# Cross-entropy on one core: the first load as two transfers of even and odd partitions, both ahead of the opening barrier, and the labels by GpSimd's queue

## The chip, the core and the metric

The kernel runs on one core of a Trainium2 chip. The metric is the device time of one launch in microseconds (us). A profile of one execution of each kernel shows the span from its first to its last instruction, some 1.8 us shorter than the device time.

## The reference

```python
batch, num_classes = 256, 32000
log_probs = logits - max(logits, axis=-1)
log_probs = log_probs - log(sum(exp(log_probs), axis=-1))
out[i] = -log_probs[i, labels[i]]            # float32, 256 numbers
```

The logits are 32.77 MB of float32, read once. Everything else is small.

## The kernel before

Two rows of the batch lie in each of the 128 partitions, one after the other, 64000 columns in all. They are loaded in 14 chunks of falling width by the sync engine's queue (SP). ScalarE takes the exponential of each chunk as it lands, with its sum as by-product.

```python
CHUNKS = [1024, 15104, 12672, 8960, 7136, 4992, 3872, 2848, ...]   # 14 in all
SLOTS = [0, 1, 2, 3, 4, 5, 2]       # the first six have buffers of their own

def load(i):
    t, base = tiles[i]
    a, b = starts[i], starts[i] + CHUNKS[i]
    nc.sync.dma_start(out=t[:, a - base:b - base], in_=flat[:, a:b])
...
first = len(set(SLOTS))             # 6
for i in range(first):
    load(i)
nc.scalar.dma_start(out=lbl[:, :], in_=...)     # labels, 2 KB, ScalarE's hardware queue
nc.gpsimd.iota(out=idx[:, :], ...)
make_identity(nc, ident[:, :])
nc.gpsimd.tensor_add(out=idx[:, :], in0=idx[:, :], in1=lbl[:, 0:2 * ROWS:2])
for r in range(ROWS):
    nc.gpsimd.indirect_dma_start(out=g[:, r:r + 1], in_=logits[:, :], ...)   # the labels' logits
```

All engines meet at a barrier before the program's body begins. A function that runs when the program is finished takes the sync engine's first load out of the body and puts it ahead of that barrier:

```python
first = next(i for i in rest if i.engine == SP and i.opcode == "DMACopy")
rest.remove(first)
at = next(k for k, i in enumerate(head) if i.engine == SP and i.opcode == "Drain")
head.insert(at, first)              # cut: the two lists are stored back
```

The softmax here doesn't subtract the row's maximum and nothing guards it: scores larger than these inputs give would overflow.

Of the kernel before, what the change touches and what calls it, by code (L numbers as in the profile page):

```python
# [9 lines left out]
P = 128  # L10
# [19 lines left out]
def begin_first_load_before_barrier(nc):  # L30


    main, body = nc.m.functions[0].blocks[:2]
    rest = list(body.instructions)
    first = next(i for i in rest if i.engine == mybir.EngineType.SP and i.opcode == "DMACopy")
    rest.remove(first)
    head = list(main.instructions)
    at = next(
        k for k, i in enumerate(head) if i.engine == mybir.EngineType.SP and i.opcode == "Drain"
    )  # L40
    head.insert(at, first)
    main.instructions = head
    body.instructions = rest

# [2 lines left out]
def kernel(  # L47
# [5 lines left out]
):  # L53
    nc = tc.nc
    nc.at_finalize(begin_first_load_before_barrier)
    B, C = logits.shape
    assert B == P * ROWS and sum(CHUNKS) == ROWS * C


    flat = logits.rearrange("(p r) c -> p (r c)", r=ROWS)  # L60
# [4 lines left out]
    at = 0  # L65
# [43 lines left out]
    def load(i):  # L109
        t, base = tiles[i]  # L110
        a, b = starts[i], starts[i] + CHUNKS[i]
        nc.sync.dma_start(out=t[:, a - base:b - base], in_=flat[:, a:b])  # L112

    seen = [0] * ROWS

    def exps(i):
        t, base = tiles[i]
        for a, b, r in pieces[i]:
            if i == last:
                acc = s_last[:, :]  # L120
            else:
                acc = parts[r][:, seen[r]:seen[r] + 1]
                seen[r] += 1
            nc.scalar.activation(  # L124
                out=t[:, a - base:b - base],
                in_=t[:, a - base:b - base],
                func=AF.Exp,
                accum_out=acc,
            )

    def log_row(r):
        nc.scalar.activation(  # L132
            out=res[0:1, r:ROWS * P:ROWS], in_=lane[r][:, :], func=AF.Ln
        )

    with tc.manual_schedule():
        first = len(set(SLOTS))
        for i in range(first):
            load(i)

        nc.scalar.dma_start(
            out=lbl[:, :], in_=bass.AP(tensor=lbl_words, offset=0, ap=[[2 * ROWS, P], [1, 2 * ROWS]])
        )
        nc.gpsimd.iota(out=idx[:, :], pattern=[[C, ROWS]], base=0, channel_multiplier=ROWS * C)  # L144
# [3 lines that stand above are left out]
            nc.gpsimd.indirect_dma_start(  # L148
                out=g[:, r:r + 1],
                out_offset=None,  # L150
                in_=logits[:, :],
                in_offset=bass.IndirectOffsetOnAxis(ap=idx[:, r:r + 1], axis=1),
            )


        done = 0
        for i in range(first, len(CHUNKS)):
            slot = SLOTS[i] if i < TAIL else TAIL_SLOT
            while done <= SLOTS[:first].index(slot):
                exps(done)  # L160
                done += 1
            load(i)
        nc.scalar.activation(out=eg[:, :], in_=g[:, :], func=AF.Exp, scale=-1.0)  # L163
        for r in range(ROWS):
            nc.vector.tensor_scalar_mul(diag[r][:, :], ident[:, :], eg[:, r:r + 1])  # L165
        for i in range(done, last):
            exps(i)
            if i == turn:
                nc.vector.reduce_sum(out=sums[:, 0:1], in_=parts[0][:, :], axis=mybir.AxisListType.X)  # L169
                nc.tensor.matmul(lane[0][:, :], sums[:, 0:1], diag[0][:, :], start=True, stop=True)  # L170
            if i == turn + 1:
                log_row(0)
            if i == WARM_FROM:
                col = parts[1][:, seen[1] - 1:seen[1]]
                for _ in range(WARM):
                    nc.tensor.matmul(warm[:, :], col, diag[0][:, :], start=True, stop=True)  # L176
        nc.vector.reduce_sum(out=sums[:, 1:2], in_=parts[1][:, :], axis=mybir.AxisListType.X)  # L177
        nc.tensor.matmul(lane[1][:, :], sums[:, 1:2], diag[1][:, :], start=True, stop=False)  # L178
        exps(last)
        nc.tensor.matmul(lane[1][:, :], s_last[:, :], diag[1][:, :], start=False, stop=True)  # L180
        log_row(1)
        nc.sync.dma_start(
            out=out.rearrange("(a n) -> a n", a=2), in_=res[0:1, :].rearrange("o (a n) -> o a n", a=2)
        )
# [30 lines left out]
```

## Time and profile before

| | us |
|---|---|
| device time, median of six runs | 84.47 (84.29 to 84.98) |
| span of the profile | 82.6 |
| first load issued, first 4 KB packet moves | 0.00, 1.03 |
| second load (15104 columns) issued | 0.81 |
| exponentials of the first three chunks begin | 3.70, 21.58, 36.72 |
| ScalarE busy | 58.4 |

How to read it: up to 36.7 us the kernel is one stream of loads, after that ScalarE is nearly always busy, and what ScalarE does then starts when the stream's first large chunks have landed. The list of DMA issues gives, for each load, its size and the time from issue to landing (last number, us):

```profile
x<-in_logits_dram SPq DMA_DIRECT2D x1, 7552.0 KB, 20.7
...
x<-in_logits_dram SPq DMA_DIRECT2D x1, 512.0 KB, 3.7
```

The timeline of the sync engine in two short windows gives the issues themselves (start, us, what):

```profile
0.00 0.40 SPq L112 DMA_DIRECT2D x<-in_logits_dram  x1
...
0.81 0.80 SPq L112 DMA_DIRECT2D x<-in_logits_dram  x2
```

The first issue takes 0.40 us. The second row is two issues, the second and the third load, back to back.

### The profile page before, as it was taken

How to read it: one execution, taken by the hardware profiler on the slowest of the kernel's cores; microseconds unless marked ns; L12 is line 12 of the kernel's file. 1: busy time of each engine (PE TensorE's matmuls, PEld its weight loads, DVE VectorE, ACT ScalarE, POOL GpSimd, SP SyncE). 2: the span in 40 equal slices, each digit the busy share in tenths (PEclk: the TensorE clock that was granted, in tenths of full speed). 3: DMA queues.
4: the chain of work that ended last, by engine and by line, in shares of the span. 5: the costliest groups of instructions: out<-in, count | busy, mean ns of one | idle time of the engine just before them, and what ended most of it. 6: DMA issues, size and time to landing. Idle time of an engine off the chain costs nothing.

```text
span 82.6 us, 174 instructions
## 1 busy us (share of the span) xinstructions
PE 6.0 (7%) x30; PEld 2.9 (4%) x30; DVE 0.8 (1%) x4; ACT 58.4 (71%) x34; POOL 3.0 (4%) x10
## 2 busy tenths in 40 slices
PE   0000000000000000000000002000000000008970
PEld 0000000000000000000000000000000000005620
DVE  0000000000000000000000020000000000000000
ACT  6230000000599999629999999989999999999970
POOL 3000000000370000000000000000000000000000
PEclk9999999999999999999999999999999999999998
DMA  4999999678999999979899799999999999999800
GB/s 73 649 469 469 469 469 439 264 322 381 491 516 540 418 393 393 393 330 504 382 452 486 318 415 443 443 405 435 464 395 450 397 431 423 419 408 408 325 0 0
DMA packets 2226, 32.77 MB, mean 397 GB/s; under 512 B 433, under 2 KB 434, under 8 KB 1202
## 3 DMA queue, kind: packets, MB, share of 16 engines
q1 hardware_dynamic: 2018, 32.77, 93.4%
q10 hardware_dynamic: 144, 0.00, 0.1%
q0 software_dynamic: 64, 0.00, 0.1%
HBM read 32.77 MB, written 0.00 MB: 397 GB/s over the span
## 4 chain that ended last, share of the span: by engine, by line
DMA 43%; ACT 39%; issue 13%; PE 0%; SPq 0%; another core or an unknown queue 0%
DMA x<-in_logits_dram 43%; ACT x L124 27%; ACT x_tail L124 12%; ACT res L132 1%; PE lane L180 0%; SPq L112 0%; ACT eg L163 0%
## 5 line engine op out<-in xcount | busy, mean ns | idle before, releaser
L124 ACT ACTIVATE x<-x 128x1024 f32<-128x1024 f32 (+7 forms) x8 | 46.4, 5794 | 20.9 <-DMA x<-in_logits_dram 20.9
L124 ACT ACTIVATE x_tail<-x_tail 128x2848 f32<-128x2848 f32 (+6 forms) x7 | 9.8, 1404 | 0.0
L176 PE MATMUL warm<-diag,parts 128*1 128x128 f32 x24 | 4.7, 382 | 23.2 <-ACT x_tail L124 23.2
L170 PE MATMUL lane<-diag,sums 128*1 128x128 f32 x2 | 0.6, 397 | 50.8 <-DVE sums L169 50.8
L176 PEld LDWEIGHTS warm<-diag,parts 128*1 128x1 f32 x24 | 2.7, 115 | 25.4 <-ACT x_tail L124 23.7
L148 POOL DMA_INDIRECT g<-in_logits_dram,idx x2 | 2.1, 1036 | 0.6 <-issue 0.3
L170 PEld LDWEIGHTS lane<-diag,sums 128*1 128x1 f32 x2 | 0.1, 80 | 50.8 <-DVE sums L169 50.8
L103 ACT ACT_TABLE_LOAD x1 | 1.3, 1283 | 0.8 <-PEq L199 0.8
L124 ACT ACTIVATION_READ_ACCUMULATOR x<-x 128x1 f32 x8 | 1.5, 186 | 0.0
L124 ACT ACTIVATION_READ_ACCUMULATOR x_tail<-x_tail 128x1 f32 x7 | 1.3, 185 | 0.0
L165 DVE TENSOR_SCALAR diag<-ident,eg 128x128 f32<-128x128 f32 x2 | 0.5, 282 | 47.8 <-ACT eg L163 47.8
L146 POOL TENSOR_TENSOR idx<-idx,lbl 128x2 int32<-128x2 int32 x1 | 0.2, 193 | 20.2 <-DMA lbl<-in_labels_dram 20.2
L132 ACT ACTIVATE res<-lane 1x128 f32<-1x128 f32 x2 | 0.5, 265 | 0.5 <-PE lane L180 0.5
L177 DVE TENSOR_REDUCE sums<-parts 128x1 f32<-128x10 f32 x1 | 0.2, 163 | 28.4 <-ACT x_tail L124 28.4
L180 PE MATMUL lane<-diag,s_last 128*1 128x128 f32 x2 | 0.4, 270 | 0.1
L178 PE MATMUL lane<-diag,sums 128*1 128x128 f32 x2 | 0.4, 270 | 0.1
masks.py:199 POOL TENSOR_SCALAR_AFFINE_SELECT ident<-ident 128x128 f32<-128x128 f32 x1 | 0.3, 292 | 0.1
masks.py:197 POOL MEMSET ident<- 128x128 f32 x1 | 0.2, 194 | 0.0
L163 ACT ACTIVATE eg<-g 128x2 f32<-128x2 f32 x1 | 0.2, 187 | 0.0
L169 DVE TENSOR_REDUCE sums<-parts 128x1 f32<-128x4 f32 x1 | 0.2, 156 | 2.3 <-ACT x L124 2.3
L144 POOL IOTA idx<- 128x2 int32 x1 | 0.1, 120 | 0.5 <-POOLq L199 0.5
L199 POOL MEMSET const-uint8-127<- 128x1 uint8 x1 | 0.1, 118 | 0.0
(5 smaller groups left out, 0.5 us busy)
## 6 DMA issues: line engine op xcount, KB each, us to landing
x<-in_logits_dram SPq DMA_DIRECT2D x1, 7552.0 KB, 20.7
x<-in_logits_dram SPq DMA_DIRECT2D x1, 6336.0 KB, 35.5
x<-in_logits_dram SPq DMA_DIRECT2D x1, 4480.0 KB, 45.6
x<-in_logits_dram SPq DMA_DIRECT2D x1, 3568.0 KB, 53.6
x<-in_logits_dram SPq DMA_DIRECT2D x1, 2496.0 KB, 59.0
x<-in_logits_dram SPq DMA_DIRECT2D x1, 1936.0 KB
x_tail<-in_logits_dram SPq DMA_DIRECT2D x1, 1424.0 KB, 21.7
x_tail<-in_logits_dram SPq DMA_DIRECT2D x1, 1072.0 KB, 23.8
```

Source lines behind the costliest of these rows:

```text
L103: nc.scalar.preload_act_table_set("natural_log_exp_and_others")
L124: nc.scalar.activation(out=t[:, a - base:b - base], in_=t[:, a - base:b - base], func=AF.Exp, accum_out=acc,)
L132: nc.scalar.activation(out=res[0:1, r:ROWS * P:ROWS], in_=lane[r][:, :], func=AF.Ln)
L146: nc.gpsimd.tensor_add(out=idx[:, :], in0=idx[:, :], in1=lbl[:, 0:2 * ROWS:2])
L148: nc.gpsimd.indirect_dma_start(out=g[:, r:r + 1], out_offset=None, in_=logits[:, :], in_offset=bass.IndirectOffsetOnAxis(ap=idx[:, r:r + 1 ...
L163: nc.scalar.activation(out=eg[:, :], in_=g[:, :], func=AF.Exp, scale=-1.0)
L165: nc.vector.tensor_scalar_mul(diag[r][:, :], ident[:, :], eg[:, r:r + 1])
L169: nc.vector.reduce_sum(out=sums[:, 0:1], in_=parts[0][:, :], axis=mybir.AxisListType.X)
L170: nc.tensor.matmul(lane[0][:, :], sums[:, 0:1], diag[0][:, :], start=True, stop=True)
L176: nc.tensor.matmul(warm[:, :], col, diag[0][:, :], start=True, stop=True)
L178: nc.tensor.matmul(lane[1][:, :], sums[:, 1:2], diag[1][:, :], start=True, stop=False)
L180: nc.tensor.matmul(lane[1][:, :], s_last[:, :], diag[1][:, :], start=False, stop=True)
```

## The change

The intent: bring the first data in sooner by giving the 16 DMA engines half-loads to begin with, and bring the labels sooner by a queue of their own. The first load becomes two transfers of 64 partitions, even and odd; both are put ahead of the barrier; the labels go by GpSimd's software queue.

```diff
-    first = next(i for i in rest if i.engine == SP and i.opcode == "DMACopy")
-    rest.remove(first)
+    first = [i for i in rest if i.engine == SP and i.opcode == "DMACopy"][:2]
+    for i in first:
+        rest.remove(i)
...
-    head.insert(at, first)
+    head[at:at] = first
...
-        nc.sync.dma_start(out=t[:, a - base:b - base], in_=flat[:, a:b])
+        step = 2 if i == 0 else 1
+        for p in range(step):
+            nc.sync.dma_start(out=t[p:P:step, a - base:b - base], in_=flat[p:P:step, a:b])
...
-        nc.scalar.dma_start(
+        nc.gpsimd.dma_start(
             out=lbl[:, :], ...
```

More of the change, by code (lines that the diff above doesn't have):

```diff
@@ L34, in begin_first_load_before_barrier @@
     rest = list(body.instructions)
-    first = next(i for i in rest if i.engine == mybir.EngineType.SP and i.opcode == "DMACopy")
-    rest.remove(first)
+    first = [i for i in rest if i.engine == mybir.EngineType.SP and i.opcode == "DMACopy"][:2]
+    for i in first:
+        rest.remove(i)
     head = list(main.instructions)
```

## The prediction

> **What bounds the kernel now.** I read the chain of waits first, then the timeline, then the table of stretches, and only then the waits and issues of the small label transfer. The chain in order of time:
>
> ```profile
> 22 pieces in order of time: start us, us, what
> 0.81 0.33 SPq L112
> 1.14 0.05 issue
> 1.19 35.51 DMA x<-in_logits_dram
> 36.70 0.02 issue
> ...
> 55.51 0.25 another core or an unknown queue
> ...
> 69.93 9.84 ACT x_tail L124 x14
> ```
>
> Up to 36.70 us the chain is the stream of loads. After that it is ScalarE, exponential after exponential, with one more short wait at 55.51 us. The timeline shows the same waits at the instruction that waits:
>
> ```profile
> 3.70 1.06 ACT L124 ACTIVATE x<-x 128x1024 f32<-128x1024 f32 x1 [1.62 <-DMA x<-in_logits_dram]
> 21.58 12.79 ACT L124 ACTIVATE x<-x 128x15104 f32<-128x15104 f32 x1 [16.72 <-DMA x<-in_logits_dram]
> 36.72 10.76 ACT L124 ACTIVATE x<-x 128x12672 f32<-128x12672 f32 x1 [2.26 <-DMA x<-in_logits_dram]
> 55.78 6.15 ACT L124 ACTIVATE x<-x 128x7136 f32<-128x7136 f32 x1 [0.27 <-DMA x<-in_logits_dram]
> ```
>
> The number in brackets is idle time just before the instruction. The first exponential ends at about 4.8 us, and the engine then stands for 16.7 us until the second chunk lands: when the first chunk lands is of no use in itself. What counts is when the 15104, 12672 and 7136 columns have landed, and those three are points on one stream. Check: columns 1024 to 16128 are 7.73 MB, which landed in 21.58 - 3.70 = 17.9 us, 432 GB/s; the next 6.49 MB took 36.72 - 21.58 = 15.1 us, 429 GB/s; the next 8.24 MB took 19.06 us, 432 GB/s. The stream runs at one speed and never stops, so a stream that starts d earlier brings each of these landings, and the end, forward by d. The other way round as well.
>
> So the question is the start of the stream. The table of stretches (columns: window, its length, five engines' busy time, clock, DMA share, GB/s) shows it:
>
> ```profile
> 0.00:1.00 1.00, 0.00 (x0) 0.00 (x0) 0.00 (x0) 0.20 (x1) 0.29 (x6) 1.00 0.00 0
> 1.00:1.50 0.50, 0.00 (x0) 0.00 (x0) 0.00 (x0) 0.50 (x1) 0.42 (x3) 1.00 1.13 131
> 1.50:2.00 0.50, 0.00 (x0) 0.00 (x0) 0.00 (x0) 0.50 (x1) 0.05 (x1) 1.00 0.58 156
> 2.00:2.50 0.50, 0.00 (x0) 0.00 (x0) 0.00 (x0) 0.09 (x1) 0.00 (x0) 1.00 0.97 385
> 5.20:7.40 2.20, 0.00 (x0) 0.00 (x0) 0.00 (x0) 0.00 (x0) 0.00 (x0) 1.00 0.95 412
> ```
>
> Nothing moves for 1.0 us, and then the rate is low for another 1.0 to 1.5 us. From 1.0 to 2.5 us the three rows give 0.5 x (131 + 156 + 385) = 336 KB; at 432 GB/s it would have been 648 KB, so the ramp costs (648 - 336) / 432 = 0.72 us. (Later rows count a 60 KB packet where it starts, so the half-microsecond rows from 2.5 to 3.5 us are not rates.) The packet records of the trace say what the ramp is: the first 4 KB packets of the first load start from 1.03 us on, spread over about 0.4 us, and last 0.16 to 1.0 us each; from about 2.1 us on a packet lasts 0.159 us and they follow each other without a gap. The first packets of the second load start between 2.84 and 3.35 us, engine by engine, and the engine that begins it last ends it last: eight packets of 2.23 us make 3.35 into 21.2 us, and the exponential starts at 21.58. The latest engine of the ramp sets the time.
>
> **What the Trainium skill says.** "DMA: Bandwidth & Descriptors", section "Rules for kernel authors", says of two transfers to disjoint partition halves not to bother, as both are spread over the same 16 engines and serialize. That speaks against a gain in bandwidth, and I expect none: the stream already holds 432 GB/s here. The same page, "Queues, rings and completion order", says that a DMA engine takes turns between queues packet by packet. The trace agrees: the labels, 128 packets of 16 bytes on ScalarE's queue, lie one between each two 60 KB packets, and so land only with the second chunk (below). "Perfetto Trace Analysis", section "DMA Optimizations", says that splitting transfers may let some start sooner where DMA engines are idle; the first 2 us here are such a place. Its lifecycle of a hardware-generated DMA, section "DMA Instruction — HWDGE (DVE, Sync)", says that the generator is locked for one instruction at a time and shared between sequencers; no row of this trace shows that directly.
>
> **The change part by part.**
>
> 1. Two issues ahead of the barrier. In the instruction records the first issue takes 0.00 to 0.40 us, the sequencer's drain 0.45 to 0.58, the barrier's release reaches it at 0.73, and the second load is issued at 0.81. The timeline's issues on that queue last 0.33 to 0.50 us. A second issue therefore adds about 0.40 us (0.35 and a gap of 0.05), and every engine that waits at the barrier leaves it about 0.40 us later. ScalarE's table load (0.80 to 2.09) moves to about 1.20 to 2.49, still before any data at 3.4 to 3.7: free. GpSimd's small work moves likewise: free.
>
> 2. The second load is issued at about 1.21 instead of 0.81. From the first load, issue to first packet is 1.03 us, so its descriptors would be there at about 1.21 + 1.03 = 2.24 us. They are needed when the first engine has finished the first load, 2.84 us now. Slack 0.60 us, so the later issue is hidden, unless the ramp shortens by more than that.
>
> 3. The ramp. Each half has 64 rows of 4 KB, four per engine instead of eight. The first packet still pays issue and first-read latency: no change there. What can shrink is the spread of starts, if the generator serves engine after engine: half the descriptors, half of 0.4 us, so 0.2 us at most for the last engine. The second half is issued at about 0.45 and its descriptors come about 1.03 later, at 1.48; four packets of 0.159 keep an engine busy for 0.64 us after the first arrives, so there is no hole. Against the gain, the slow first packets last up to 1.0 us whatever follows them, and the slowest engine now (first packet 1.26 to 2.26 us) is late mostly by that. I take 0.15 us as gain.
>
> 4. The labels. Now:
>
> ```profile
> lbl<-in_labels_dram ACTq DMA_DIRECT2D x1, 2.0 KB, 20.9
> 21.78 0.19 POOL L146 TENSOR_TENSOR idx<-idx,lbl 128x2 int32<-128x2 int32 x1 [20.23 <-DMA lbl<-in_labels_dram]
> 22.27 1.13 POOL L148 DMA_INDIRECT g<-in_logits_dram,idx  x1 [0.30 <-POOL idx L146]
> ```
>
> The gathers then land 8.6 to 11.0 us after issue, at about 33 us; the exponential of their result runs at 47.48. So there are 14 us of slack already, and landing earlier is worth nothing on the path. On GpSimd's queue the issue should cost about what a gather costs it, 0.94 to 1.13 us, on an idle engine. The gathers' data come in 32-byte packets, 8 elements each, one per engine and gather; if the labels are packed so too, they need one or two turns of 2.23 us rather than eight, and should land near 5 to 8 us. Removed from ScalarE: one issue of 0.37 us beside the table load, worth nothing. Removed from the engines: eight turns of about 3 ns each (60 KB packets start every 2.232 us and last 2.229), 0.02 us.
>
> Sum: 84.38 - 0.15 (ramp) - 0.02 (label packets) + 0 (barrier, hidden) = 84.21, and I say 84.25, as part of the ramp's gain may not reach the slowest engine.
>
> **The rivals.**
> - Nothing happens: the ramp is read latency of the first packets and not the supply of descriptors. For it: the long first packets, and the rule on halves. Against: starts spread over 0.4 us. It makes 84.4.
> - The barrier's delay takes over: the second load's descriptors come later than I work out (a 60 KB row may take longer than a 4 KB one to begin), and the stream has a hole at 2.8 to 3.2 us. Against: the slack of 0.60 us. At most the whole 0.40 us: 84.8.
> - A larger gain: the ramp is slow because the generator is shared. The second load's issue (0.81 to 1.14) and the labels' issue on the other queue (0.83 to 1.20) fall just before and into it; the change moves the one later and the other off the hardware generator. If the whole 0.72 us of ramp were won: 83.7.
> - The labels by software come so late that the exponential of the gathered values at 47.5 us waits and ScalarE stands in its busy stretch. This would need over 14 us of delay. Unlikely.
>
> **Range and chances.** The three runs before lie within 0.23 us. From 0.5 us won to 0.35 us lost with most weight near 0.1 to 0.2 won: 83.9 to 84.65, predicted 84.25. A change of 2% is 1.69 us, more than the whole start of the stream can give (its ramp is 0.72 us) and four times what the barrier can take: within 2% at 0.98, 0.01 to either side.
>
> **What would show it.** In the changed profile: the second load's issue at about 1.2 us; the first exponential at about 3.55 instead of 3.70; the second, third and 7136-column exponentials each earlier by the same 0.1 to 0.2 us as one another, and the end too; the label sum on GpSimd at 5 to 8 us instead of 21.78, the gathers landed before 22 us, with no trace in the end. I am wrong on the ramp if the 15104-column exponential starts at 21.5 or later or before 21.2 us; wrong on the slack if the engines show a gap between the first and second load; and wrong on the whole view if the end moves by another amount than that exponential does.

## The result, and the profile after

| | before | after |
|---|---|---|
| device time, median of six runs, us | 84.47 | 87.33 (87.08 to 87.71) |
| span of the profile, us | 82.6 | 85.5 |
| second load issued, us | 0.81 | 1.83 |
| its exponential begins, us | 21.58 | 24.64 |

The change is slower. The ratio of the times is 1.033 (95% interval 1.029 to 1.037). Here and below a ratio is the mean time of one kernel's runs over that of the other's in the same rounds, so it is not quite the ratio of the medians quoted. Executions over 1.5% slower than the fastest of the same kernel are left out of the means.

First the chain of waits of the changed kernel, the lines that answer to those of before:

```profile
1.83 0.37 SPq L116
2.20 0.05 issue
2.25 37.36 DMA x<-in_logits_dram
39.62 0.02 issue
...
58.43 0.25 another core or an unknown queue
```

It is the same chain in the same order, begun 1.02 us later, and its DMA piece is 37.36 us long instead of 35.51. So a late start explains only a third of the loss. Next, the exponentials in the timeline, with ScalarE's idle time before each in brackets:

```profile
3.68 1.06 ACT L128 ACTIVATE x<-x 128x1024 f32<-128x1024 f32 x1 [0.56 <-DMA x<-in_logits_dram]
24.64 12.79 ACT L128 ACTIVATE x<-x 128x15104 f32<-128x15104 f32 x1 [19.81 <-DMA x<-in_logits_dram]
39.64 10.76 ACT L128 ACTIVATE x<-x 128x12672 f32<-128x12672 f32 x1 [2.12 <-DMA x<-in_logits_dram]
58.70 6.15 ACT L128 ACTIVATE x<-x 128x7136 f32<-128x7136 f32 x1 [0.27 <-DMA x<-in_logits_dram]
```

The first chunk landed when it did before (3.68 against 3.70 us). The second is 3.06 us later, and the two behind it 2.92 us later each, as is the end (the span grew by 2.9 us). By rates: the second chunk's 7.73 MB took 24.64 - 3.68 = 20.96 us, 369 GB/s where it had been 432; the third's 6.49 MB took 15.00 us, 433 GB/s, and the next 8.24 MB 19.06 us, 432 GB/s. All of the loss is made between 3.7 and 24.6 us, in the second load.

The issues of the sync engine, again from three short windows of its timeline:

```profile
0.00 0.55 SPq L116 DMA_DIRECT2D x<-in_logits_dram  x1
...
0.60 0.58 SPq L116 DMA_DIRECT2D x<-in_logits_dram  x1
...
1.83 0.37 SPq L116 DMA_DIRECT2D x<-in_logits_dram  x1
```

The two transfers of 64 partitions take longer to issue than the one of 128 before: 0.55 and 0.58 us against 0.40. The instruction records add that the sync engine's drain behind them takes 0.37 us instead of 0.13, and that the barrier lets it go at 1.76 us instead of 0.73.

The table of stretches (window, length, busy time of five engines, clock, DMA share, GB/s) shows the ramp:

```profile
1.00:1.50 0.50, 0.00 (x0) 0.00 (x0) 0.00 (x0) 0.00 (x0) 0.00 (x0) 1.00 0.61 82
1.50:2.00 0.50, 0.00 (x0) 0.00 (x0) 0.00 (x0) 0.17 (x1) 0.00 (x0) 1.00 0.46 115
2.00:2.50 0.50, 0.00 (x0) 0.00 (x0) 0.00 (x0) 0.50 (x1) 0.14 (x1) 1.00 1.00 377
```

It moved 0.5 x (82 + 115 + 377) = 287 KB by 2.5 us, against 336 KB before. The first packet moves at 1.34 us, not 1.03: the ramp got no shorter, it begins later.

The packet records of the trace show what went wrong behind it. They carry times, sizes and queues, and no engine; packets were chained to 16 engines by matching each end with the next start. Where engines stood idle, which end belongs to which start can't be told; the gaps below pair them in order (first to end, first to begin). Before, every engine went from its last 4 KB packet straight into its first 60 KB packet, between 2.84 and 3.35 us. After, seven engines do so between 3.08 and 3.27 us, and nine stand idle for 0.7 to 1.7 us first, the last until 4.95 us. The first 60 KB packets then last 2.38 to 3.02 us where they had lasted 2.23 to 2.25; full speed is back only with the third or fourth. The engine that began last began at 4.95 instead of 3.35 us, which is 1.60 us lost in the gap. Its chain of eight packets is unbroken and took 18.67 us instead of 17.85, which is 0.82 us more; it ends at 23.62 us, where before the last packet ended at 21.20. Two other engines end later still, at 24.10 and 24.17 us. Traced back, each leads to one of the labels' packets (128 bytes on the software queue), which lasted 0.60 and 0.58 us between 9.8 and 10.7 us. With the labels alone moved (section 1 below) all 16 such packets last 0.015 us, so they are slow here along with the stream; 24.17 - 23.62 = 0.55 us of the landing in this profile goes with them. Together 2.97 us.

The labels landed earlier, as intended, to no effect:

```profile
13.38 0.19 POOL L150 TENSOR_TENSOR idx<-idx,lbl 128x2 int32<-128x2 int32 x1 [9.54 <-DMA lbl<-in_labels_dram]
```

### The profile page after: what moved, and what is told of

It reads as the page before. It is cut to its first block, busy times and chain, and to the rows that moved or that the text cites. A ratio compares the mean times of both kernels' runs of the same rounds, so it can differ in the third digit from the quotient of the medians.

```text
span 85.5 us, 177 instructions
## 1 busy us (share of the span) xinstructions
PE 6.1 (7%) x30; PEld 3.0 (4%) x30; DVE 0.8 (1%) x4; ACT 58.4 (68%) x34; POOL 3.7 (4%) x11
## 4 chain that ended last, share of the span: by engine, by line
DMA 44%; ACT 38%; issue 13%; PE 0%; SPq 0%; another core or an unknown queue 0%
DMA x<-in_logits_dram 44%; ACT x L128 26%; ACT x_tail L128 12%; ACT res L136 1%; PE lane L184 0%; SPq L116 0%; ACT eg L167 0%
## 5 line engine op out<-in xcount | busy, mean ns | idle before, releaser
L145 POOL DMA_DIRECT2D lbl<-in_labels_dram x1 | 0.7, 712 | 1.9 <-POOLq L203 1.9
```

Source lines behind the costliest of these rows:

```text
L145: nc.gpsimd.dma_start(out=lbl[:, :], in_=bass.AP(tensor=lbl_words, offset=0, ap=[[2 * ROWS, P], [1, 2 * ROWS]]))
```

## The experiments

Three theories. A: the second load is issued late, and what is late is lost. B: the labels on the software queue disturb the start. C: transfers of 64 partitions burden whatever makes descriptors (the orders that tell a DMA engine what to move), and delay what comes behind. A fourth, D, came up on the way: the loads behind the second one compete with it. All were run three rounds against the kernel before unless said otherwise; the median of before beside them is 84.6 us in sections 1 to 3. In sections 4 to 6 it is 84.5, or 84.3 for two runs on another chip (the fill of 448 columns, and the second load between the halves). All results were correct.

### 1. The parts by themselves

The halves alone: the labels go back to ScalarE's queue.

```diff
-        nc.gpsimd.dma_start(out=lbl[:, :], ...
+        nc.scalar.dma_start(out=lbl[:, :], ...
```

> The changed kernel with the labels back on ScalarE's hardware queue: the two halves alone. Theory A (late second load: two issues hold the sync engine 1.2 us, the second load is issued 1.0 us later, its descriptors reach some engines after these ran dry): 85.9 to 86.2 us, that is the 1.6 us of gaps before the latest engine's first 60 KB packet, and no slow label packets. Theory B (labels by the software queue cause the gaps and the slow first packets): 84.3 to 84.7. If the two are independent, this run and the next should add up to the +2.9 us.

Measured 87.32 us, ratio 1.034. The labels alone, with the first load whole, are the other half:

> The kernel before with only the labels moved to GpSimd's queue. Theory A: 84.4 to 84.6, at most 0.2 us for the label packets. Theory B: 86 us or more, with 60 KB packets of 2.4 to 3.0 us at the start of the second load and label packets of 0.2 to 0.6 us.

Measured 84.53 us, ratio 1.000 (0.997 to 1.002). The labels land at 10.48 us instead of 21.78, and that is worth nothing:

```profile
10.48 0.20 POOL L146 TENSOR_TENSOR idx<-idx,lbl 128x2 int32<-128x2 int32 x1 [7.68 <-DMA lbl<-in_labels_dram]
```

So theory B falls, and the halves carry the whole loss, whichever queue the labels use; A had put this run at 86.2 at most, so A was short too. Next, only the even half ahead of the barrier, the odd one behind it:

```diff
-    ... i.opcode == "DMACopy"][:2]
+    ... i.opcode == "DMACopy"][:1]
```

> The changed kernel, with only the even half ahead of the barrier and the odd half as the first issue behind it. The barrier should come at about 0.9 us, the second load be issued at about 1.5 us rather than 1.83. Theory A: the gaps shrink by about 0.3 us, so 86.8 to 87.1. Theory B (labels): unchanged, 87.3.

Measured 86.15 us, ratio 1.020. Better than expected, though the second load is issued at 1.72 us, hardly sooner, and the first exponential waits until 5.22 us: the odd half itself comes late. It was issued at 1.19 us:

```profile
1.19 0.48 SPq L116 DMA_DIRECT2D x<-in_logits_dram  x1
```

By the packet records it moves only from 2.5 us on, its early packets last up to 1.39 us, and its last one ends at 4.83 us. The second load then follows without a gap and nearly at full rate. So what came late here is the transfer issued second, not the second load. Then blocks of partitions, 0 to 63 and 64 to 127, in place of even and odd:

```diff
-            nc.sync.dma_start(out=t[p:P:step, a - base:b - base], in_=flat[p:P:step, a:b])
+            lo, hi = p * P // step, (p + 1) * P // step
+            nc.sync.dma_start(out=t[lo:hi, a - base:b - base], in_=flat[lo:hi, a:b])
```

> The changed kernel with partitions 0 to 63 and 64 to 127 as the two transfers in place of even and odd. If the stride of the partitions makes the issues slow (0.55 and 0.58 us against 0.40), the issues fall to about 0.40 us each, the second load goes out about 0.3 us earlier and the time to about 87.0. If it is the number of issues that costs, 87.3.

Measured 87.11 us, ratio 1.032, with issues of 0.55 and 0.58 us as for even and odd. The stride is not the cause. The long issue isn't a matter of 64 partitions alone either: a load of 128 partitions issued directly behind a half took 0.58 us in the run above and 0.59 with three ahead (below), and only 0.41 behind a whole first load.

### 2. Is it the late second load?

The kernel before with its whole first load, and an idle fill on VectorE ahead of the barrier, so that the barrier alone is late:

```diff
+    idle = small.tile([P, 1280], F32, name="idle")
+    nc.vector.memset(idle[:, :], 0.0)      # moved ahead of the barrier
```

> The kernel before, whole first load, labels on ScalarE, with one idle fill on VectorE ahead of the barrier, so that the barrier and the second load come about 1.0 us later while the sync engine still makes one issue. Theory A (it is the late issue of the second load alone): gaps of 0.7 to 1.7 us ahead of the second load and 86.5 to 87.3 us. Theory C (transfers of 64 rows burden the descriptor generator, and that is what delays the second load): no gaps or gaps below 0.4 us, 84.4 to 84.8 us.

Measured 86.36 us, ratio 1.019. The gaps are there (five engines wait 0.7 to 1.5 us), and the first 60 KB packets take 2.8 to 3.2 us. So a late second load costs this much without any halves; C alone can't be. (The fill delays all that stands behind the barrier, not the second load alone; the run with two loads ahead, below, separates the two.) Then the changed kernel with the second load ahead of the barrier too:

```diff
-    ... i.opcode == "DMACopy"][:2]
+    ... i.opcode == "DMACopy"][:3]
```

> The changed kernel with the second load ahead of the barrier too, so that it is issued at about 1.24 us instead of 1.83. Theory A: the gaps shrink by about 0.6 us and fewer 60 KB packets are slow: 85.3 to 86.3 us. Theory C: no better than 86.8.

Measured 87.44 us, ratio 1.036. The second load was issued 0.60 us sooner and nothing was won:

```profile
1.23 0.59 SPq L116 DMA_DIRECT2D x<-in_logits_dram  x1
```

A, in the form that each 0.1 us of delay costs its 0.1 us, falls. The same with a whole first load, two transfers ahead:

> The kernel before with its whole first load and the whole second load ahead of the barrier, labels on ScalarE: the second load is issued at about 0.45 instead of 0.81 us, the third at about 1.2 as now. Both theories: no gap to remove before, so 84.3 to 84.6. If it is faster by over 0.2 us, the second load is already late in the kernel before; if slower by over 0.3, an issue ahead of the barrier has a cost of its own, or the third load's lateness counts too.

Measured 84.67 us, ratio 1.000. An issue ahead of the barrier costs nothing in itself, and the second load gains nothing from going out at 0.45 us instead of 0.81. The barrier let the sync engine go at 1.19 us here, later than the 1.06 us of the fill of 640 columns (section 4), which lost 2.3 us: a late barrier by itself costs nothing. Last, more columns in the first load, so that the second is needed later:

```diff
-    1024, 15104, ...
+    2048, 14080, ...
```

> The changed kernel with 2048 columns in the first load and 14080 in the second (from 1024 and 15104): the first load lasts 1.2 us longer, so the engines need the second load's descriptors 1.2 us later, while the issues stay where they are. Theory A: most gaps (0.7 to 1.7 us) close and the time falls to 84.6 to 85.6. Theory C: the cost of the halves stays, 86.5 to 87.3.

Measured 85.99 us, ratio 1.016. No engine has a gap any more, and half of the loss is gone; but most of the first large packets still last 2.2 to 3.0 us where 2.08 is their normal time. Gap and slow packets are two things, and a later need cures only the first.

### 3. Is it the loads behind the second one?

Theory D was tried by holding the third to sixth load back until the first exponential had run: a one-column write by ScalarE into the third chunk's buffer makes them wait, by true dependence.

```diff
-        for i in range(first):
+        for i in range(2):
             load(i)
...
-        done = 0
+        exps(0)
+        done = 1
+        nc.scalar.activation(out=tiles[2][0][:, 0:1], in_=parts[0][:, 0:1], func=AF.Exp, scale=0.0)
+        for i in range(2, first):
+            load(i)
```

> The changed kernel, but the third to sixth loads are held back until the first exponential has run (about 4.8 us; the third is needed at about 22 us). Theory D (the second load is not late by its own issue, but its descriptors reach the engines in competition with those of the four loads issued behind it): the gaps ahead of the second load and the slow 60 KB packets go, 84.4 to 85.2 us. Theory A (the second load's own issue is late): gaps of 0.7 to 1.7 us stay, 86.0 to 87.3. A slow spell that moves to 5 to 8 us would say that issuing four loads while the engines stream costs by itself.

Measured 87.00 us, ratio 1.028: gaps of up to 2.1 us with nothing behind the second load in the queue. The control, the same hold in the kernel before:

> The kernel before with the same hold: the control. Theories A and D: no gap before and none now, 84.4 to 84.8. If issuing four large loads into the running stream costs by itself: slow 60 KB packets from 5 us on and 85 us or more.

Measured 84.46 us, ratio 0.998, with the four loads issued into the running stream at 5.1 to 6.8 us. And the same hold with the late barrier:

> The late barrier with the single first load (86.36 us), and the same hold. Theory D: the gaps of 0.7 to 1.5 us go, 84.4 to 85.2. Theory A: they stay, 85.8 to 86.4.

Measured 86.29 us, ratio 1.022. D falls in all three. One look without rounds had the 4992-column load (20 KB rows) second:

> The changed kernel with the 4992-column load (rows of 20 KB) issued second, ahead of the 15104 columns. Only the start is looked at; ScalarE waits longer for the 15104 columns. If the delay of the second load grows with the bytes of its rows, the gaps ahead of the 20 KB packets are a third of those ahead of the 60 KB packets, below 0.6 us; if not, they are again up to 1.7 us.

93.45 us, as ScalarE waits for the large chunk. Ten engines begin their first 20 KB packet by 3.3 us; the other six not before 4.6 us, at least 1.3 us after the last 4 KB packet ended. That is as with 60 KB packets: the delay is not a matter of the second load's bytes. (One execution, of which only the start is read.)

### 4. A sweep of the second load's issue

Since 1.23 and 1.83 us cost alike, and 0.45 and 0.81 nothing, the idle fill of the late barrier was shortened, with the whole first load: 640, 960 and 448 columns instead of 1280.

> Whole first load, idle fill half as long: the second load is issued at about 1.25 us, as with three transfers ahead of the barrier (1.23, 87.4 us). If the time of issue alone decides: gaps of over 0.5 us and 86 us or more. If the halves ahead of it are the burden: no gaps, 84.4 to 84.8.

> Whole first load, the second issued at about 1.53 us. Between the run above and the late barrier (1.81 us, 86.4): if delivery gets slow only once the engines move data at full rate, from about 2.0 us on, a step: gaps and 85.5 to 86.4 here. If the cost is just the delay in excess of slack, it grows evenly from issue to issue: 84.8 to 85.6.

> Whole first load, idle fill short enough for the second load to be issued at about 0.95 us, just before the first packet moves (1.0 us). A step at the first packet: 84.4 to 84.8, no gaps. A step nearer to 0.81: 86.3 or more. Between the two (85.0 to 86.0): a slope over some 0.3 us.

The issue of the second load and the DMA piece behind it in the chain of waits, for the fills of 448, 640, 960 and 1280 columns in turn:

```profile
0.94 0.33 SPq L119
1.27 0.05 issue
1.32 35.61 DMA x<-in_logits_dram
```

```profile
1.14 0.33 SPq L119
1.47 0.05 issue
1.52 37.75 DMA x<-in_logits_dram
```

```profile
1.47 0.33 SPq L119
1.80 0.05 issue
1.85 37.03 DMA x<-in_logits_dram
```

```profile
1.81 0.33 SPq L119
2.14 0.05 issue
2.19 36.63 DMA x<-in_logits_dram
```

In each fence the first line is the second load's issue, and the last runs from the third load's issue, directly behind it, to the landing of the third chunk. A second load issued 0.20 us later, at 1.14 instead of 0.94, makes that piece 2.1 us longer; still later issues don't make it longer still. The times say the same:

| second load issued at, us | first load | median, us | ratio |
|---|---|---|---|
| 0.45 (two loads ahead) | whole | 84.67 | 1.000 |
| 0.94 (fill 448) | whole | 84.69 | 1.003 (0.998 to 1.007) |
| 1.14 (fill 640) | whole | 86.78 | 1.027 |
| 1.47 (fill 960) | whole | 86.56 | 1.026 |
| 1.81 (fill 1280) | whole | 86.36 | 1.019 |
| 1.23 (three ahead) | halves | 87.44 | 1.036 |
| 1.83 (the change) | halves | 87.33 | 1.033 |

With a whole first load it is a step, and it lies between 0.94 and 1.14 us. The first packet of a whole first load moves at 1.01 to 1.03 us, which invites the reading that the issue must come before that moment. The halves speak against it: there the first packet moves at 1.32 to 1.33 us, and transfers issued before it, at 1.19 (the odd half behind the barrier, section 1) and 1.23 us (three ahead, section 2), came late all the same.

### 5. The step with halves

If the step is what the halves fell over, the same three transfers ahead of the barrier must do better when the second load is issued between the halves, ahead of the step:

```diff
-    head[at:at] = first
+    head[at:at] = [first[0], first[2], first[1]]
```

> Three transfers ahead of the barrier as in the run that took 87.4 us, but in the order even half, second load, odd half, so that the second load is issued at about 0.61 us instead of 1.23. The odd half then lands behind the second load, at about 21 us, which is early enough for the exponential of the first chunk. If the step between 0.81 and 1.14 us decides: 84.4 to 85.2. If two halves ahead of the barrier cost by themselves: 86.5 or more.

Measured 85.32 us, ratio 1.009 (1.005 to 1.013), just above the range expected, against 87.44 us for the other order. The list of DMA issues, the second load's line, with the second load last of the three and then between the halves:

```profile
x<-in_logits_dram SPq DMA_DIRECT2D x1, 7552.0 KB, 23.4
```

```profile
x<-in_logits_dram SPq DMA_DIRECT2D x1, 7552.0 KB, 21.4
```

It was issued at 1.23 us in the first and at 0.61 us in the second, so it landed at 24.6 and 22.0 us. No engine stands idle for long (0.35 us at most). The 0.8 us that stay are in the stream too: the third chunk lands at 37.5 us, against 36.7 before. Another way to the same end is to issue the second load from ScalarE's queue ahead of the barrier, beside the halves:

> The changed kernel with the second load issued from ScalarE's queue ahead of the barrier, at about 0.1 to 0.5 us. The first load then shares the engines with it and lands at up to 20 us, which is early enough for its 1.2 us exponential. If only the second load's lateness costs: 84.3 to 84.9. If halves cost by themselves: 85.5 or more.

Measured 85.08 us, ratio 1.007, also just above the range expected, with the issue at 0.12 us. Part of this may be that two queues now share each engine at the start; but most of the loss is gone here as well.

### 6. A version that might beat both

The first chunk is of no use to ScalarE by itself, so it was merged with the second into one load of 16128 columns (five rounds; the tables of buffers behind it, cut here, were adapted):

```diff
-    1024, 15104, 12672, ...
+    16128, 12672, ...
```

> The kernel before with the first two loads merged into one of 16128 columns, issued ahead of the barrier. Nothing behind it can be late: the third chunk is needed at 21 us. No gap between loads; the ramp is paid inside the first large packet; the exponentials lose one instruction. 84.0 to 84.5, that is 0 to 0.4 us faster than before.

Measured 84.89 us, ratio 1.005 (1.003 to 1.006): slower by 0.4 us, where 0 to 0.4 us faster was expected. The first packet of each engine, now 64.5 KB, lasts 2.8 to 3.3 us where later ones last 2.38, and the merged chunk lands at 22.0 us. The small first load earns its place. No version tried beats the kernel before.

## Why the prediction was wrong

The view of the kernel held. The second chunk's exponential moved by 3.06 us and the end by 2.9, and behind that exponential the path has the same pieces as before. The sign and the size were wrong, and the time lies 2.7 us above the range.

- **Part 1, the cost of an issue: wrong.** It took a second issue at 0.35 us and a gap. Measured are 0.55 and 0.58 us, with a drain 0.24 us longer, so that the second load went out at 1.83 instead of the 1.21 us predicted.
- **Part 2, the slack: this is the step that failed.** It took 1.03 us from issue to first packet, measured on the first load when nothing else moved, and applied it to the second, so that the later issue would be hidden. Its own sign of being wrong on the slack, a gap between the first and second load, came true. Issued at 1.14 us, with a whole first load, even earlier than the predicted 1.21, the second load was not there at 2.2 us: some engines began it at 4.5 to 5.2 us, and 2.3 us were lost. The slack was not 0.60 us but between 0.13 and 0.33 us of issue time (0.94 fine, 1.14 not), and to overrun it cost 1.7 to 2.3 us with a whole first load, not the overrun.
- **Part 3, the ramp: wrong, small.** No 0.15 us was won. The first exponential came at 3.68 us, not 3.55, as the first packets came 0.31 us later.
- **Part 4, the labels: right in worth, wrong in time.** They landed at 13.4 us, not 5 to 8, and the gathers after about 24 us, not before 22. Moving them is worth 0.0 us, as the labels alone show.
- **The rivals.** The second named the right place, a hole at the end of the first load by the late second one, but bounded its cost by the barrier's delay, 0.40 us. It is not bounded by it: on the engine that began last the gap alone was 1.60 us, and slow packets added 0.82 us. That the issue of a half takes longer and delays the barrier by 1.02 us was in no rival.

What stays open is why there is a step. Shown: with a whole first load, a second load issued by 0.94 us is ready when needed; issued at 1.14 to 1.81 us, it reaches the last engine 2.7 to 4.0 us after its issue, and its first packets last up to 3.6 us where 2.23 is normal. With halves, moving its issue from 1.23 to 0.61 us takes the ratio from 1.036 to 1.009. Ruled out: the labels' queue, the loads behind it, the bytes of its rows, the stride of the partitions, an issue ahead of the barrier as such, and a late barrier as such. Not shown: that the moment of the first packet sets the step. That descriptors are delivered slowly while the engines ramp up would fit, but no record here shows descriptors. Open too is why halves lose 0.5 to 1 us more than a late barrier does (slow label packets were 0.55 us of it in one profile, but without them on that queue the time was the same), and why a half, and what is issued directly behind it, takes longer to issue.

## What to carry to other kernels

At the start of a stream, what must not be late is the second large load: put its issue right behind the first (here 0.94 us after the first issue was early enough, 1.14 us was not), and put nothing in front of it. Before splitting a load, measure what an issue of the new shape costs, and what the engine that issues it holds up. A latency that was measured on an idle machine is no estimate for the same thing on a busy one, and slack that is overrun can cost far more than the overrun.

## What the Trainium skill lacked or had wrong

- "DMA: Bandwidth & Descriptors", "Rules for kernel authors": the advice against transfers to disjoint partition halves is right, but for its reason, that they serialize, the outcome would be about even. Here the halves alone lost 2.7 us of 84.6 (ratio 1.034).
- No page has the step: with a whole first load and the second issued at 0.94 us nothing was lost, at 1.14 us 2.3 us were.
- No page gives that two first issues of 64 partitions each take longer on the hardware queue (0.55 and 0.58 us) than those of 128 (0.40 and 0.41 us), with a drain of 0.37 us instead of 0.13 behind them.
- "Perfetto Trace Analysis", "DMA Optimizations", says that splitting may let some transfers start sooner, and names engines that are generally idle. Here they are idle only in the first us, and there the split made the first packet later, 1.34 us instead of 1.03.
- "DMA: Bandwidth & Descriptors", "SWDGE vs HWDGE vs iDMA", has hardware generation as the faster setup. The issue agrees (0.37 us on ScalarE's queue, 0.71 on GpSimd's), but setup doesn't decide the landing: 128 labels of 16 bytes behind a running stream landed at 10.5 us by the software queue, with eight of them in one packet, and at 21.8 us by the hardware queue, with one in each.
